# Down-projection's weights scaled and combined ahead, during the FFN, and read back from memory as seven finished quarters

## The chip, the cores and the metric

One core of a Trainium2 chip runs the kernel. The time is the device time of one execution in microseconds. Three runs of the kernel before gave 1437.60, 1434.86 and 1437.55 us, a median of 1437.55 us. One more execution was profiled; its own numbers stand further down.

## What is computed

One decoder layer on x of 1024 tokens by 1024 features: attention of two head groups, an output projection with a residual, then the FFN and a last norm. Only the end of it is touched:

```
h2 = rmsnorm(x, g_ffn) * (1 + sc2) + sh2
gate, up = split(h2 @ w_gu, 2)                    # w_gu: 1024 x 5632
x = x + ga2 * ((silu(gate) * up) @ w_down)        # w_down: 2816 x 1024, ga2: one factor per output column
return rmsnorm(x, g_final)
```

The factor ga2 scales output columns, so it can be multiplied into w_down's columns ahead of the product. All is in float32; every matrix product is made of three matmuls on a high and a low part of each operand.

## The kernel before

**The FFN.** Row blocks f = 0 to 21 (22 blocks of 128 of the 2816 hidden features). Each f makes seven products of quarter size instead of eight (a Strassen-Winograd form): 7 products of 4 x 3 matmuls of 128x512, so 84 per f. `ff_prep(f)` loads the two weight tiles of f (SP queue, L1247, four raw buffers in turn in f16), makes the combinations t1 to t4 on POOL (L1278, L1279, L1282, L1286, into f8) and splits seven operands into high (ACT, L1240) and low (DVE, L1241) parts, in twenty pages used in turn. The products are taken out of PSUM by DVE (L1298 to L1312, one input in PSUM) and ACT (L1297); PSUM has four banks "mm", two "tp" and two "o", and four of the seven products use "mm", two "tp", one "o". POOL makes the two gated results (L1310, L1313) and sends them to memory (L1311, L1314, `spill_g`).

**The down-projection.** First `plain()`, the row blocks 0 and 1 (96 matmuls). Then three chunks `CH` of 3, 3 and 4 pairs of row blocks, each again as seven products (numbered 1, 2, 7, 5, 6, 4, 3 in order of time) of 4 tiles x 3 matmuls x 3 or 4 pairs. `g_quarter` loads quarters of the gated result, `w_quarter` loads quarters b11, b21, b12, b22 of w_down (SP queue, L1353) and multiplies them by ga2 (`scaled`, L1398, on POOL or DVE as the letters of `EN` say). `sub` (L1451, POOL or DVE by `EN`) makes the combinations of both sides: per chunk four of the gated result and four of the weights. `operands` splits the two operands of a product into a high part (ACT, L1365) and a low part (DVE, L1366) in a ring of two places, so the operands of one product are split while PE works on the product before. DVE takes the products out of PSUM and adds them up (L1376).

**What sets the order.** The statements are written in one order; a scheduler that replays the program against its own idea of how long things take decides in which order each engine gets its instructions. On the chip each engine and each DMA queue then runs its list strictly in that order.

In the diff, G is POOL, V is DVE, A is ACT and nc.sync is SP's DMA queue. `mrs` are two buffers of the output projection, f2 one more; all three are unused in the FFN before.

## Time and profile before

| | |
|---|---|
| median of three runs | 1437.55 us |
| the profiled execution, its own time | 1437.92 us |
| its span, first to last instruction | 1436.1 us |
| norms end, FFN begins | about 705 to 755 us |
| FFN at an even pace | about 760 to 1146 us |
| first matmul of the down-projection | 1165.36 us |
| its last matmul | about 1418 us |
| last norm's outputs written | to 1436 us |

PE is the engine that multiplies, with its weight loads (PEld) beside it; busy times overlap between engines, so the busy share of one engine says little without what it waits for. A row of the timeline has a start, a duration that includes any blocking inside the instruction, and in brackets the idle time before it with what ended it. "Granted clock" is 1.00 at 2.4 GHz and 0.50 at 1.2 GHz.

### The profile page before, as it was taken

Reading aid. Unit: us, or ns where it says so; the run is one execution under the profiler, and the core shown is the slowest. Engines: PE = TensorE matmul, PEld = TensorE weight load, DVE = VectorE, ACT = ScalarE, POOL = GpSimd, SP = SyncE. Lnnn points to the kernel's source line nnn. Section 1 sums busy time; section 2 is a strip of 40 time slices with the busy share of each in tenths; the row PEclk is TensorE's granted clock in tenths of the full one; section 3 lists DMA queues with packets and bytes.
Section 4 is the critical chain, followed back from the end, with each engine's and each line's share of the span. In section 5 each row is a group of like instructions: output and inputs, shape, how many; then the busy total and the mean of one; then the engine's idle time right before and its main releaser. Section 6 shows DMA issues by size and latency. Waiting matters only on the chain.

```text
span 1436.1 us, 20358 instructions
## 1 busy us (share of the span) xinstructions
PE 1297.0 (90%) x7477; PEld 1033.9 (72%) x7477; DVE 1016.3 (71%) x1754; ACT 598.8 (42%) x1217; POOL 674.9 (47%) x454
## 2 busy tenths in 40 slices
PE   2999898999878899999869999999999998888894
PEld 0566776798666677787748888888888886766773
DVE  4136899999887477644987545554545569999997
ACT  3435546461456565613763333333333223223334
POOL 1650311324330598122676444445544436487865
PEclk9999898999989999999979999999999999999997
DMA  9723124233311444273423222222223281404004
GB/s 240 238 75 117 30 67 125 91 101 95 126 52 54 147 142 119 76 227 114 161 79 98 89 88 81 66 88 81 81 88 96 87 322 46 154 23 154 0 1 118
DMA packets 133018, 152.11 MB, mean 106 GB/s; under 512 B 9715, under 2 KB 95540, under 8 KB 132918
## 3 DMA queue, kind: packets, MB, share of 16 engines
q1 hardware_dynamic: 122160, 129.56, 29.8%
q0 software_dynamic: 4672, 15.73, 2.9%
q10 hardware_dynamic: 6086, 5.52, 1.5%
q8 instruction: 59, 0.97, 0.3%
q14 instruction: 41, 0.34, 0.1%
HBM read 115.65 MB, written 34.60 MB: 105 GB/s over the span
## 4 chain that ended last, share of the span: by engine, by line
PE 49%; DVE 29%; POOL 8%; DMA 6%; issue 5%; ACT 3%; SPq 1%; DVEq 0%; ACTq 0%; POOLq 0%
DVE score L620 7%; PE mm L1258 6%; PE mm L1256 6%; PE mm L1257 6%; PE tp L1256 3%; PE tp L1258 3%; PE tp L1257 3%; PE mm L366 3%; PE mm L368 3%; PE mm L367 2%; PE o L762 2%; DVE yacc L1376 2%; PE mm L762 2%; PE tp L762 2%; DVE score L424 2%
## 5 line engine op out<-in xcount | busy, mean ns | idle before, releaser
L1240 ACT ACTIVATE wo<-f 128x512 fp32r<-128x512 f32 x124 | 78.0, 631 | 178.0 <-PE mm L1258 78.8
L1241 DVE TENSOR_TENSOR wo<-f,wo 128x512 fp32r<-128x512 f32 x124 | 102.7, 831 | 43.8 <-ACT wo L1240 41.9
L366 PE MATMUL mm<-hh,wl 128*128 128x512 f32 (+2 forms) x288 | 111.7, 389 | 0.0
L367 PE MATMUL mm<-hh,wh 128*128 128x512 f32 (+2 forms) x288 | 111.2, 387 | 0.0
L368 PE MATMUL mm<-hl,wh 128*128 128x512 f32 (+2 forms) x288 | 108.1, 385 | 0.0
L214 POOL TENSOR_SCALAR wh<-wraw 128x1024 fp32r<-128x1024 f32 (+1 forms) x20 | 20.3, 1032 | 132.6 <-PE mm L368 82.3
L366 PE MATMUL mm<-wo,wo 128*128 128x512 f32 x148 | 59.0, 398 | 10.1 <-DVE wo L1366 10.1
L215 POOL TENSOR_TENSOR wl<-wraw,wh 128x1024 fp32r<-128x1024 f32 (+1 forms) x22 | 52.6, 2410 | 29.8 <-ACT ry L144 29.7
L366 PEld LDWEIGHTS mm<-hh,wl 128*128 128x128 f32 (+1 forms) x288 | 54.4, 189 | 15.2 <-issue 2.8
L368 PEld LDWEIGHTS mm<-hl,wh 128*128 128x128 f32 (+1 forms) x288 | 53.7, 188 | 14.0 <-issue 2.2
L367 PEld LDWEIGHTS mm<-hh,wh 128*128 128x128 f32 (+1 forms) x288 | 54.6, 190 | 11.5 <-issue 1.1
L368 PE MATMUL mm<-wo,wo 128*128 128x512 f32 x148 | 56.9, 393 | 1.7 <-DVE wo L1366 1.7
L367 PE MATMUL mm<-wo,wo 128*128 128x512 f32 x148 | 58.2, 393 | 0.0
L793 ACT ACTIVATE ttB<-ttB,mn 128x128 f32<-128x128 f32 (+7 forms) x64 | 49.1, 768 | 15.5 <-DVE mn L789 14.9
L1366 DVE TENSOR_TENSOR wo<-f,wo 128x1536 fp32r<-128x1536 f32 (+1 forms) x17 | 55.1, 3246 | 0.0
L1310 POOL TENSOR_TENSOR f<-f 128x512 f32<-128x512 f32 x15 | 19.8, 1322 | 74.2 <-ACT f L1309 74.2
L366 PE MATMUL mm<-wo,ml 128*128 128x512 f32 x128 | 51.6, 403 | 1.8 <-DVE ml L1109 1.8
L762 PE MATMUL tp<-ident,ttB 128*128 128x128 f32 x288 | 43.6, 294 | 10.2 <-ACT ptB L808 9.7
L620 DVE TENSOR_SCALAR_CACHE_REDUCE score<-kl,sc 128x1024 bf16<-128x1024 uint16 (+2 forms) x48 | 52.3, 1140 | 0.0
L620 DVE TENSOR_SCALAR_CACHE_REDUCE score<-ka,sc 128x768 bf16<-128x768 int16 (+2 forms) x48 | 52.3, 1139 | 0.0
L367 PE MATMUL mm<-wo,mh 128*128 128x512 f32 x128 | 51.0, 398 | 0.0
L368 PE MATMUL mm<-wo,mh 128*128 128x512 f32 x128 | 50.9, 398 | 0.0
(469 smaller groups left out, 4238.7 us busy)
## 6 DMA issues: line engine op xcount, KB each, us to landing
f<-in_w_gu_dram SPq DMA_DIRECT2D x44, 512.0 KB, 3.8
spg<-f POOLq DMA_DIRECT2D x44, 256.0 KB, 2.8
wraw<-in_w_in_dram SPq DMA_DIRECT2D x21, 512.0 KB, 4.0
f<-spg SPq DMA_DIRECT2D x33, 256.0 KB, 3.0
va<-in_w_ada_dram SPq DMA_DIRECT2D x16, 512.0 KB, 4.2
wlm<-in_w_ada_dram SPq DMA_DIRECT2D x32, 256.0 KB, 2.7
f<-in_w_down_dram SPq DMA_DIRECT2D x23, 256.0 KB, 3.1
more<-in_w_down_dram SPq DMA_DIRECT2D x21, 256.0 KB, 5.4
```

The source lines that it names most:

```text
L215: G.tensor_tensor(lo, raw, hi.bitcast(F32), op=OP.subtract)
L366: PE.matmul(p, al, bh, start=(j == 0), stop=False)
L367: PE.matmul(p, ah, bh, start=False, stop=False)
L368: PE.matmul(p, ah, bl, start=False, stop=(j == n - 1))
L620: V.tensor_scalar(mask(t, u), keys[:, seg[t]], z[:, i:i + 1], 0.0, op0=OP.is_lt, op1=OP.add, accum_out=cnt[:, i:i + 1])
L762: pe_last[0] = op(*args, **kw)
L1240: A.activation(h_, src, AF.Copy)
L1241: V.tensor_tensor(l_, src, h_.bitcast(F32), op=OP.subtract)
L1256: PE.matmul(p, w[1][:, k], a[0][:, k], start=(k == 0), stop=False)
L1257: PE.matmul(p, w[0][:, k], a[0][:, k], start=False, stop=False)
L1258: PE.matmul(p, w[0][:, k], a[1][:, k], start=False, stop=(k == 3))
L1366: V.tensor_tensor(l_, x, h_.bitcast(F32), op=OP.subtract)
```

## The change

During the FFN, from f = 1 on, row pairs 1 to 10 of w_down are treated in 40 units (`units`: pair j, and one of four strips h of 128 columns of each half). A unit is loaded by two DMAs of 128 KB on SP's queue into one of three buffers (`wslot`: two of `mrs`, and f2) with four blocks b12, b22, b11, b21 of 128x128; DVE multiplies it by ga2 in two instructions of 128x256; three of the blocks go to `spill_w` (192 KB); POOL makes T3, T2, T1, T4 in place with four subtractions of 128x128, of which the first overwrites b11; the four go to `spill_w` (256 KB). Then the buffer may be loaded again. The down-projection reads b11, b21, T3, T1, T2, T4 and b22 of each chunk, as seven finished quarters, through four buffers in turn (`wq`). `scaled` is gone; of `sub` the four on the gated result remain.

```diff
+    spill_w = {j: dram.tile([P, 7, 512], F32, name=f"spw{j}") for j in range(1, NF // 2)}
...
+    wbuf = [y.rearrange("p a b -> p (a b)") for y in mrs] + [f2]
+    units = [(j, h) for j in range(1, NF // 2) for h in range(4)]
...
+    def w_load(s):
+        if s < len(units):
+            j, h = units[s]
+            for i, u in enumerate((1, 0)):
+                nc.sync.dma_start(wslot(s)[0][:, i], wdn[2 * j:2 * j + 2, :, u * 512 + h * P:u * 512 + h * P + P]
+                                  .rearrange("r p c -> p r c"))
+    def w_step(s):
+        w_load(s + 1)
+        if 1 <= s <= len(units):
...
+            G.tensor_tensor(b11, b12, b11, op=OP.subtract)
+            G.tensor_tensor(b12, b22, b12, op=OP.subtract)
+            G.tensor_tensor(b22, b22, b11, op=OP.subtract)
+            G.tensor_tensor(b21, b21, b22, op=OP.subtract)
+            nc.sync.dma_start(spill_w[j][:, 3:7, h * P:h * P + P], b)
+        if s < len(units):
+            j, h = units[s]
+            for i, u in enumerate((1, 0)):
+                v = wslot(s)[0][:, i]
+                V.tensor_tensor(v, v, gate2[:, u:u + 1, h * P:h * P + P].to_broadcast([P, 2, P]), op=OP.mult)
+            nc.sync.dma_start(spill_w[j][:, 0:3, h * P:h * P + P], wslot(s)[1][:, 1:4])
...
     for f in range(NF):
+        if f:
+            w_step(2 * f - 2)
...
+        if f:
+            w_step(2 * f - 1)
+        else:
+            w_load(0)
...
-    EN = ("GVVVVGGGGGGG", "GGVGGGGGGGGG", "GGGGGGGGGGGG")
+    EN = ("VGGG", "GGGG", "GGGG")
+    wq = [[f6[1], more[:, 13:14]], [more[:, 0:4]], [more[:, 4:8]], [f16[:, 4:8]]]
+    w_todo = [(n, c) for c in CH for n in ("b11", "b21", "T3", "T1", "T2", "T4", "b22")]
+    def w_quarter():
+        name, (j0, j1) = w_todo[nw[0]]
+        nw[0] += 1
+        return quarter(wq[(nw[0] - 1) % 4], lambda j: spill_w[j0 + j][:, w_at[name]], j1 - j0)
...
-    def scaled(q, cs, eng, n):
-        for (v,) in parts(n, q):
-            eng.tensor_tensor(v, v, ga[:, 1:2, cs].to_broadcast([P, v.shape[1], 512]), op=OP.mult)
...
-        sub(b11, b12, b11)
-        sub(b12, b22, b12)
-        sub(b11, b22, b11)
-        sub(b21, b21, b11)
-        o4 = operands(g22, b21)
+        o4 = operands(g22, t4)
```

**SP's queue in the FFN.** In the kernel before, it holds the weight loads (f_6484 is f16, the raw buffers) and nothing else up to the 43rd of the 44 loads; the row ahead of them is the last load of the norms:

```order
L1169 DMA f_6484<-spy_112 128x1024
L1247 DMA f_6484<-in_w_gu_dram 128x8x128 x43
L1353 DMA f_6484<-spg_114 128x512
L1247 DMA f_6484<-in_w_gu_dram 128x8x128
```

In the changed kernel (f16 is f_6494) the same queue carries the units, whose buffers are mr_4722, mr_4723 and f_6500 (f2), and spw is `spill_w`. Twelve rows of the middle of the FFN:

```order
L1248 DMA f_6494<-in_w_gu_dram 128x8x128 x2
L1318 DMA spw_136<-mr_4723 128x4x128
L1305 DMA mr_4723<-in_w_down_dram 128x2x128 x2
L1318 DMA spw_137<-mr_4722 128x4x128
L1318 DMA spw_137<-f_6500 128x4x128
L1248 DMA f_6494<-in_w_gu_dram 128x8x128
L1324 DMA spw_137<-mr_4723 128x3x128
L1305 DMA mr_4722<-in_w_down_dram 128x2x128 x2
L1305 DMA f_6500<-in_w_down_dram 128x2x128 x2
L1324 DMA spw_138<-mr_4722 128x3x128
L1324 DMA spw_137<-f_6500 128x3x128
L1248 DMA f_6494<-in_w_gu_dram 128x8x128
```

What moved: each weight load of the FFN now stands behind loads and stores of units, and all 40 units stand ahead of the last 18 of the 44 weight loads.

**POOL and DVE in the FFN.** POOL's list for one f in the kernel before (f_6485 is f8, f_6486 and f_6487 are f6):

```order
L1282 TENSOR_TENSOR f_6485<-f_6484 128x512
L1278 TENSOR_TENSOR f_6485<-f_6484 128x512
L1279 TENSOR_TENSOR f_6485<-f_6484,f_6485 128x512
L1286 TENSOR_TENSOR f_6485<-f_6484,f_6485 128x512
L1310 TENSOR_TENSOR f_6487<-f_6487 128x512
L1311 DMA spg_116<-f_6487 128x512
L1313 TENSOR_TENSOR f_6486<-f_6486 128x512
L1314 DMA spg_116<-f_6486 128x512
```

POOL in the changed kernel, where f_6495 is f8:

```order
L1314 TENSOR_TENSOR mr_4722<-mr_4722 128x128
L1314 TENSOR_TENSOR f_6500<-f_6500 128x128
L1279 TENSOR_TENSOR f_6495<-f_6494 128x512
L1315 TENSOR_TENSOR mr_4722<-mr_4722 128x128
L1315 TENSOR_TENSOR f_6500<-f_6500 128x128
L1280 TENSOR_TENSOR f_6495<-f_6494,f_6495 128x512
L1316 TENSOR_TENSOR mr_4722<-mr_4722 128x128
L1316 TENSOR_TENSOR f_6500<-f_6500 128x128
L1287 TENSOR_TENSOR f_6495<-f_6494,f_6495 128x512
L1317 TENSOR_TENSOR mr_4722<-mr_4722 128x128
L1317 TENSOR_TENSOR f_6500<-f_6500 128x128
```

DVE in the changed kernel (f_6496 and f_6497 are f6; wo and ml are pages), from behind the multiplications of one pair of units to the first of the next:

```order
L1338 TENSOR_TENSOR f_6497<-mm,f_6497 128x512
L1242 TENSOR_TENSOR wo_6499<-f_6495,wo_6499 128x512
L1340 TENSOR_TENSOR f_6497<-mm,f_6497 128x512
L1242 TENSOR_TENSOR wo_6499<-f_6494,wo_6499 128x512
L1343 TENSOR_TENSOR f_6496<-tp,f_6497 128x512
L1344 TENSOR_TENSOR f_6497<-tp,f_6497 128x512
L1242 TENSOR_TENSOR ml_4725<-f_6494,mh_4724 128x512
L1347 TENSOR_TENSOR f_6497<-o,f_6497 128x512
L1242 TENSOR_TENSOR ml_4727<-f_6495,mh_4726 128x512
L1323 TENSOR_TENSOR mr_4723<-mr_4723,ga 128x256 x2
L1351 TENSOR_TENSOR f_6497<-mm,f_6497 128x512
L1323 TENSOR_TENSOR mr_4722<-mr_4722,ga 128x256
```

What moved: the subtractions of two units stand between POOL's t1 to t4 of an f, and DVE's multiplications of units between the products that it takes out of PSUM. From the first multiplication of the tenth unit to the last of the fortieth, DVE's list holds eight f.

**POOL at the first chunk of the down-projection.** Before (f_6487 and more hold weight quarters, f_6484 is f16):

```order
L1398 TENSOR_TENSOR f_6487<-f_6487,ga 128x1536
L1451 TENSOR_TENSOR more<-f_6487,more 128x1536
L1398 TENSOR_TENSOR more<-more,ga 128x512
L1451 TENSOR_TENSOR f_6486<-f_6486,more 128x1536
L1451 TENSOR_TENSOR f_6484<-more,f_6484 128x1536
L1451 TENSOR_TENSOR f_6485<-f_6485,f_6484 128x1536
L1451 TENSOR_TENSOR f_6484<-f_6487,f_6484 128x1536
L1451 TENSOR_TENSOR more<-more,f_6484 128x1536
L1398 TENSOR_TENSOR f_6484<-f_6484,ga 128x1536
```

After (the last of the FFN, then the subtractions on the gated result alone):

```order
L1350 DMA spg_134<-f_6497 128x512
L1352 TENSOR_TENSOR f_6496<-f_6496 128x512
L1353 DMA spg_134<-f_6496 128x512
L1493 TENSOR_TENSOR f_6496<-f_6496,more 128x1536
L1493 TENSOR_TENSOR f_6494<-more,f_6494 128x1536
L1493 TENSOR_TENSOR f_6495<-f_6495,f_6494 128x1536
L1493 TENSOR_TENSOR f_6494<-f_6494,f_6496 128x1536
L1493 TENSOR_TENSOR f_6496<-f_6496,more 128x1536
```

What moved: the multiplications by ga2 (L1398) and the subtractions of weight quarters are gone from POOL's list, which has 13 subtractions left for the three chunks.

## Rows read from the trace of the kernel before

**Rows 1.** stages: span (us), busy PE, PEld, DVE, ACT, POOL; clock, DMA share, GB/s

```profile
705.00:755.00 50.00, 33.52 (x140) 25.65 (x139) 45.49 (x62) 33.63 (x71) 36.38 (x26) 0.80 0.35 105
760.00:1146.00 386.00, 386.00 (x1669) 313.76 (x1668) 201.83 (x278) 121.97 (x198) 189.40 (x162) 1.00 0.27 84
...
1165.00:1187.00 22.00, 22.00 (x99) 18.20 (x98) 17.37 (x16) 1.16 (x1) 7.79 (x5) 1.00 1.01 374
1187.00:1245.00 58.00, 47.50 (x187) 37.96 (x186) 57.95 (x46) 18.10 (x16) 33.71 (x9) 0.88 0.21 70
```

**Rows 2.** PE's waits, 1150 us to the end: us in total, times, longest

```profile
PE tp L366 <- DVE A11l L1366: 14.8, 4, 6.1
PE mm L366 <- DVE wo L1366: 10.1, 4, 3.9
PE tp L368 <- DVE AS2l L1366: 3.8, 2, 3.1
PE mm L368 <- DVE wo L1366: 1.7, 1, 1.7
```

**Rows 3.** the same columns as the first group, 5 us around long waits

```profile
1200.00:1205.00 5.00, 5.00 (x12) 3.95 (x13) 5.00 (x6) 1.63 (x2) 2.60 (x2) 0.50 0.01 3
...
1225.00:1230.00 5.00, 4.77 (x12) 3.80 (x13) 5.00 (x8) 0.08 (x1) 3.51 (x1) 0.56 0.47 157
```

**Rows 4.** PE in time: first and thirteenth matmul of the down-projection; start, us

```profile
1165.36 0.39 PE L366 MATMUL mm<-AS2h,A11l 128*128 128x512 f32 x1
...
1168.08 0.39 PE L366 MATMUL tp<-AS2h,A11l 128*128 128x512 f32 x1
```

**Rows 5.** DVE in time, down-projection: start, us, engine, line, what

```profile
1193.11 1.74 DVE L1366 TENSOR_TENSOR AS2l<-more,AS2h 128x1536 fp32r<-128x1536 f32 x1
1194.78 4.99 DVE L1366 TENSOR_TENSOR A11l<-f,A11h 128x1536 fp32r<-128x1536 f32 x1
...
1225.10 3.67 DVE L1376 TENSOR_TENSOR yacc<-mm,yacc 128x512 f32<-128x512 f32 x6
```

**Rows 6.** POOL in time, the same stretch

```profile
1182.35 3.49 POOL L1398 TENSOR_TENSOR f<-f,ga 128x1536 f32<-128x1536 f32 x1 [12.43 <-DMA f<-in_w_down_dram]
1193.40 4.74 POOL L1451 TENSOR_TENSOR more<-f,more 128x1536 f32<-128x1536 f32 x1 [7.57 <-DVE f L1451]
...
1223.64 4.87 POOL L1451 TENSOR_TENSOR more<-more,f 128x1536 f32<-128x1536 f32 x1
```

**Rows 7.** DVE's instructions of L1366 alone, in one stretch

```profile
1187.00:1418.00 231.00, 133.94 (x42) 0.96 0.17 57
```

**Rows 8.** instructions of L1451 alone, DVE's and then POOL's

```profile
1187.00:1418.00 231.00, 3.48 (x2) 109.14 (x26) 0.96 0.17 57
```

**Rows 9.** instructions of L1398 alone, DVE's and then POOL's

```profile
1187.00:1418.00 231.00, 6.29 (x3) 35.57 (x8) 0.96 0.17 57
```

**Rows 10.** PE in time, FFN: first matmuls of two neighbouring products

```profile
1045.82 0.39 PE L1256 MATMUL mm<-AS4h,wo 128*128 128x512 f32 x1
...
1048.61 0.39 PE L1256 MATMUL mm<-A11h,wo 128*128 128x512 f32 x1
```

**Rows 11.** POOL's groups in the FFN: busy us, mean ns, idle before

```profile
L1279 POOL TENSOR_TENSOR f<-f,f 128x512 f32<-128x512 f32 x19 | 25.0, 1315 | 1.5
...
L1313 POOL TENSOR_TENSOR f<-f 128x512 f32<-128x512 f32 x13 | 22.5, 1729 | 0.3
```

**Rows 12.** DMA issues: count, KB each, median us to landing

```profile
f<-in_w_gu_dram SPq DMA_DIRECT2D x44, 512.0 KB, 3.8
...
spg<-f POOLq DMA_DIRECT2D x44, 256.0 KB, 2.8
...
more<-in_w_down_dram SPq DMA_DIRECT2D x21, 256.0 KB, 5.4
...
out_dram<-more SPq DMA_DIRECT2D x16, 128.0 KB, 2.1
```

**Rows 13.** SP's issues of L1247: ns each (least, median, most), first and last start

```profile
L1247 SPq DMA_DIRECT2D f<-in_w_gu_dram x44: 367/368/373, 705.9 to 1100.2; - x44
```

More of the change, by code (lines that the diff above doesn't have):

```diff
@@ L1289, in ff_prep, with wslot @@
         return w11, w21, w1, w2, w3, w4, w22
+    wbuf = [y.rearrange("p a b -> p (a b)") for y in mrs] + [f2]
+    units = [(j, h) for j in range(1, NF // 2) for h in range(4)]
+    gate2 = ga[:, 1].rearrange("p (u c) -> p u c", u=2)
+    def wslot(s):
+        return wbuf[s % 3].rearrange("p (u r c) -> p u r c", u=2, r=2), wbuf[s % 3].rearrange("p (a c) -> p a c", c=P)
+    def w_load(s):
[7 more added lines that the diff above has]
+        if 1 <= s <= len(units):
+            j, h = units[s - 1]
+            b = wslot(s - 1)[1]
+            b12, b22, b11, b21 = [b[:, i] for i in range(4)]
+            G.tensor_tensor(b11, b12, b11, op=OP.subtract)
[9 more added lines that the diff above has]
+            nc.sync.dma_start(spill_w[j][:, 0:3, h * P:h * P + P], wslot(s)[1][:, 1:4])
+    w_at = {"b22": 0, "b11": 1, "b21": 2, "T3": 3, "T2": 4, "T1": 5, "T4": 6}
     for f in range(NF):
@@ L1322, in hybrid_block @@
     CH = [(1, 4), (4, 7), (7, 11)]
-    EN = ("GVVVVGGGGGGG", "GGVGGGGGGGGG", "GGGGGGGGGGGG")
+    EN = ("VGGG", "GGGG", "GGGG")
     more = rw.tile([P, 14, 512], F32, name="more")
-    dq = {"g11": [f16[:, 0:4]], "b11": [f16[:, 4:8]], "g12": [f8], "b21": [more[:, 0:4]], "b12": [more[:, 4:8]],
-          "g22": [more[:, 8:12]], "g21": [f6[0], more[:, 12:13]], "b22": [f6[1], more[:, 13:14]]}
+    dq = {"g11": [f16[:, 0:4]], "g12": [f8], "g22": [more[:, 8:12]], "g21": [f6[0], more[:, 12:13]]}
+    wq = [[f6[1], more[:, 13:14]], [more[:, 0:4]], [more[:, 4:8]], [f16[:, 4:8]]]
+    w_todo = [(n, c) for c in CH for n in ("b11", "b21", "T3", "T1", "T2", "T4", "b22")]
+    nw = [0]
     u2s = [dn.tile([P, 512], F32, name=f"u2{i}") for i in range(4)]
@@ L1441, in g_quarter @@
             return quarter(dq[f"g{u + 1}{r + 1}"], lambda j: spill_g[2 * (j0 + j) + r][:, (lo, hi)[u]], j1 - j0)
-        def w_quarter(r, u):
-            q = quarter(dq[f"b{r + 1}{u + 1}"], lambda j: wdn[2 * (j0 + j) + r][:, (lo, hi)[u]], j1 - j0)
-            scaled(q, (lo, hi)[u], next(e), j1 - j0)
-            return q
         def sub(dst, x, y, op=OP.subtract):
@@ L1457, in sum_up @@
             half_final(i)
[L1459 to L1460 removed]
+        g11, b11 = g_quarter(0, 0), w_quarter()
+        g12, b21 = g_quarter(1, 0), w_quarter()
+        g21, t3 = g_quarter(0, 1), w_quarter()
+        g22, t1 = g_quarter(1, 1), w_quarter()
         o1 = operands(g11, b11)
         o2 = operands(g12, b21)
+        t2, t4 = w_quarter(), w_quarter()
         product(1, o1, first)
[L1464 removed]
         sub(g11, g11, g21)
[L1466 to L1468 removed]
         sub(g21, g21, g22, OP.add)
[L1470 removed]
+        o7 = operands(g11, t3)
+        b22 = w_quarter()
         product(2, o2, first)
[L1472 removed]
+        o5 = operands(g21, t1)
         sub(g11, g22, g11)
[L1474 removed]
         product(7, o7, first)
[L1476 removed]
+        o6 = operands(g11, t2)
         product(5, o5, first)
[L1478 removed]
         sub(g12, g12, g11)
[L1480 removed]
+        o4 = operands(g22, t4)
         product(6, o6, first, sum_up if last else None)
```

7 lines of the change are left out of this document (removed).

## Prediction

> **What bounds the kernel now.** I read the busy times by stage first. In the FFN PE is busy for all of 386.0 us at clock 1.00, with DVE at 201.8 and POOL at 189.4 us beside it [rows 1]: work put there on DVE and POOL is free as long as PE never waits. In the down-projection it is the other way round: from 1187 to 1245 us DVE is busy for 57.95 of 58 us, PE for 47.5 [rows 1]. Then PE's waits: 14.8 + 10.1 + 3.8 + 1.7 = 30.4 us in 11 waits, every one ended by DVE's low part of an operand (L1366) [rows 2]. Some of them also halve the granted clock for the next five microseconds (0.50 and 0.56, 12 matmuls in each [rows 3], where five microseconds at a full pace hold 22). A check by counting: from 1187 us to the last matmul at 1418 us are 231 us; the three chunks are 7 x 4 x 3 x (3 + 3 + 4) = 840 matmuls, and at 2.72 / 12 = 0.227 us each [rows 4] they need 190.5 us. So 40.5 us of this stage are lost.
>
> Why DVE is late is seen by laying its rows on POOL's. A low part of 128x1536 takes 1.74 us; the next one, started at 1194.78 us while POOL was in its instruction of 1193.40 us, takes 4.99 us and ends 1.63 us after POOL's [rows 5, 6]. POOL's own instruction of that size takes 3.49 us alone, and 4.74 us when DVE's low part is ahead of it [rows 5, 6]. So an instruction with two SBUF inputs on one of the two engines keeps the other's out for its whole length. DVE's additions from PSUM are not touched: six take 3.67 us, 0.61 us each, beside a POOL instruction [rows 5, 6]. In the whole stretch 42 low parts take 133.9 us [rows 7]; alone, 28 of three blocks at 1.74, 12 of four blocks at 2.3 (by size) and two small ones would take 77.5 us. 56 us of DVE's time are blocking.
>
> **The change part by part.**
>
> *The down-projection.* POOL now does 26 instructions of L1451 for 109.1 us and 8 of L1398 for 35.6 us there, 145 us [rows 8, 9]. After, 13 subtractions remain: 9 of three blocks at 3.49, two of four at 4.65 (by size), two of one block at 1.3 [rows 6, 11], 43 us. DVE also loses three multiplications (6.3 us [rows 9]). What is then late next: a product of three pairs takes PE 36 x 0.227 = 8.2 us; DVE needs two low parts and 40 / 7 additions in that time, 2 x 1.74 + 5.7 x 0.61 = 7.0 us, so it keeps up with 1.2 us to spare; with four pairs it is 10.9 against 8.1 us. A subtraction of 3.5 us that meets a low part makes it late by up to 2.3 us. If all 13 do, 27 us of waits stay (7 x 2.3 + 6 x 1.8); the low parts fill 3.5 / 8.2 = 43% of the time, so I keep 10 us. Gain: 40.5 - 10 = **30 us**, with bounds of 13 and 40 us. The loads go up from 8 to 11 quarters per chunk, but the DMA share of 0.21 there [rows 1] leaves room, and with four buffers each quarter is asked for three products ahead, some 25 us against the longest landing row of 5.4 us [rows 12]. Ahead of product 1 the DMA engines are full (share 1.01, 374 GB/s [rows 1]), and b11's last two blocks now stand behind 4.2 MB of x on SP's queue: 11 us later they land, some 10 us before product 1 begins, so I count no wait.
>
> *The start of the FFN.* The order puts the multiplications of seven units, 14 instructions, ahead of DVE's first FFN result. A 128x256 one is not in the trace; a sixth of 1.74 us and a start-up make 0.33 us (an estimate). DVE is busy for 45.5 of 50 us there [rows 1], so I take all of 14 x 0.33 as **+5 us**; bounds 0 (its idle 4.5 us) and +10 (if the 28 subtractions on POOL, busy for 36.4 of 50 us [rows 1], block as much again).
>
> *The FFN at its even pace.* By amount it fits: 40 x 2 x 0.33 = 26 us on DVE and 160 subtractions on POOL, 0.5 us each (1.315 us for 512 columns [rows 11], 3.49 for 1536 [rows 6], so 0.27 per 128 and 0.5 for the first), 80 us, over some 250 us. What may not fit is the **chain of one unit**, because the queues are in order and the scheduler packed three units into less than one f. Before a buffer can be loaded again there come, one after another: two loads (0.37 us for the first issue [rows 13] and 2.1 us for 128 KB [rows 12]), two multiplications (0.7), the store of three blocks (2.5, between 2.1 for 128 KB and 2.8 for 256 KB [rows 12]), for the first subtraction overwrites b11, then eight subtractions of two units with three of the FFN's own among them (8 x 0.5 + 3 x 1.3 = 7.9), the store of four blocks (2.8), and three issues of others on SP (1.1): 17.5 us. With 0.1 us of blocking for each of the 11 POOL instructions, 18.6 us for every three units (three buffers). The order gives them less: 31 units, the tenth to the fortieth, stand in eight f of DVE's list, and an f is 7 products of 2.79 us [rows 10], 19.5 us; 156 us for ten turns of three, 15.6 us each. So every turn falls 3.0 us behind, and 10.3 turns 31 us. Who waits: a multiplication whose load has not landed holds up DVE's list, in which the next PSUM results stand; PE feels it when a PSUM bank comes round, one f later: 19.5 - 2.8 for filling it - 0.7 for emptying it = 16 us of slack. **+15 us**. Bounds: nothing if a turn takes 17.1 us or less, +39 us at 21 us. SP's weight loads, queued behind the units' stores, have more slack: pages are split about nine products ahead, 25 us.
>
> *Small transfers.* The FFN's weight loads, in 512 B packets too, move 512 KB in 3.8 us [rows 12], and a DMA share of 0.27 moved 84 GB/s [rows 1], so 311 GB/s at a full share; the units add 31 x 0.72 MB in 156 us, 143 GB/s, a share of 0.46: no limit. The Trainium skill's page "DMA: Bandwidth & Descriptors" ("Rules for kernel authors") says to gather small transfers into large ones, and its table of measured bandwidths gives 32% of peak at 64 KB against 78% at 1 MB. By that ratio the units would take a share of up to 1.1, beyond what is left. The rows speak for the first; the other is the last rival below.
>
> *Sum against the profiled 1437.9 us*: -30 + 5 + 15 = -10 us, 1427.9 us; the median of the runs lies 0.4 us lower, so **1427.5 us**.
>
> **The rivals.**
> 1. *The units stay hidden.* If a turn takes at most 17.1 us, the 16 us of slack cover all of it: -30 + 5 = -25, 1412.5 us. For it: the unblocked sum is 17.5 us, and turns with one unit alone have no neighbour among its four subtractions. Against: blocking at the port is in every row of DVE and POOL that overlap.
> 2. *The units set the FFN's pace (slower).* The place is DVE's list between the PSUM results, the price 10.3 us for each microsecond that a turn takes above 17.1 us. It decides from 19.9 us on, where the loss of 28 + 5 us outweighs the gain. At 21 us: +39 + 5 - 30 = +14, 1451.5 us. For it: POOL waits for a store inside its list, with t1 to t4 behind it; L1313 already takes 1.73 us for 1.3 us of work [rows 11]. Against: my sum lies 1.3 us below the point.
> 3. *The down-projection keeps its waits.* The three or four subtractions per chunk hit the low parts each time, or the list places a low part late: gain 13 instead of 30, +7, 1444.5 us. Against: DVE has 22% of the stage to spare.
> 4. *The transfers crowd each other.* Landing takes the 5.4 us seen where the DMA engines were full [rows 12] instead of 2.1 to 2.8, three times per turn, +9 us: 10.3 x 12 - 16 = +108 us, some 1520 us. Against: the share of 0.27 + 0.46. (The skill's rule on small transfers would bring this about.)
>
> **How the numbers follow.** Chances: forecast 0.44 (its own range 1420 to 1436 us), rival 1 0.25, rival 2 0.21, rival 3 0.07, rival 4 0.03. Of 0.2% (about what a measurement can tell, 2.9 us) the bounds are 1434.7 and 1440.4 us. Faster: 0.37 of the forecast and all of rival 1, 0.62. Same: 0.06 of the forecast and 0.02 of rival 3, 0.08. Slower: the rest, 0.30. The range from 1411 us (most of rival 1) to 1453 us (two thirds of rival 2) leaves out about 0.2.
>
> **What would show each step.** Right: from the first chunk to the last matmul about 200 us, low parts of 128x1536 near 2 us on the mean, no clock of 0.50 there; in the FFN gaps of PE ended by DVE's PSUM results, from the third or fourth f on, ending when the fortieth unit is done, some 15 us in all, with DVE waiting for DMA landings of units. Rival 1: no PE gap in the FFN. Rival 2: gaps of 4 us and more per f, and a clock below 1.00. Rival 3: PE waits on L1366's successor above 20 us. Rival 4: unit loads landing later than 4 us. Wrong altogether would be a down-projection in which PE waits for quarters from memory.

## The result and the profile after

The changed kernel takes 1454.5 us (median of 4 runs, 1453.4 to 1457.1) where the kernel before took 1437.6 on the same chip: a ratio of 1.0113, 95% interval 1.0076 to 1.0151. It is slower, and the forecast was 1427.5 us, faster. Ten more runs of it (e11) gave 1448.8 us, a ratio of 1.004, so the loss is some 0.4% to 1.1%.

Three points in the traces cut both kernels into the pieces that the prediction had terms for: VectorE's first addition of the last norms, its first result from the FFN's PSUM, and its result of the last FFN product (line `ff_mm(w22, ...)` of the last f). Here is that last line's group in the kernel before, then in the changed one (duration in ns least/median/most, first and last start in us):

```profile
L1312 DVE TENSOR_TENSOR f<-mm,f x22: 678/691/693, 759.2 to 1165.6; 128x512 f32<-128x512 f32 x22
```

```profile
L1351 DVE TENSOR_TENSOR f<-mm,f x22: 677/688/693, 779.9 to 1217.9; 128x512 f32<-128x512 f32 x22
```

| piece, us of the profiled run | before | after | difference | forecast (bounds) |
|---|---|---|---|---|
| start to the norms' first addition | 666.7 | 673.0 | +6.3 | 0 |
| norms to the FFN's first result | 83.5 | 94.2 | +10.7 | +5 (0, +10) |
| first to last FFN result | 415.4 | 450.7 | +35.3 | +15 (0, +39) |
| last FFN result to the end | 270.5 | 233.9 | -36.6 | -30 (-40, -13) |
| span | 1436.1 | 1451.8 | +15.7 | -10 |

So the down-projection gave what was hoped and a little more, and the units cost 46 us in place of 20. The first 6.3 us lie ahead of any unit; run e11 takes them up.

Stages of the changed kernel (columns as in [rows 1]); the fourth is followed by the same stretch of the kernel before. The last two rows are of the down-projection and of its low parts; they answer to the down-projection's row in [rows 1], 52 us later since the FFN ends later, and to [rows 7]:

```profile
705.00:755.00 50.00, 26.02 (x106) 19.83 (x106) 48.73 (x68) 30.13 (x69) 37.26 (x38) 0.71 0.51 156
730.00:760.00 30.00, 14.13 (x44) 10.49 (x44) 30.00 (x41) 15.84 (x35) 24.59 (x23) 0.55 0.42 122
760.00:1146.00 386.00, 360.71 (x1512) 287.63 (x1512) 234.79 (x326) 108.84 (x188) 258.70 (x295) 0.98 0.49 144
840.00:1000.00 160.00, 136.47 (x546) 105.64 (x545) 96.61 (x144) 36.72 (x67) 114.58 (x154) 0.96 0.59 174
```

```profile
840.00:1000.00 160.00, 160.00 (x693) 130.06 (x692) 81.56 (x116) 51.18 (x83) 77.91 (x67) 1.00 0.25 80
```

```profile
1239.00:1297.00 58.00, 56.27 (x247) 46.02 (x246) 53.32 (x52) 22.14 (x18) 12.59 (x4) 1.00 0.50 164
```

```profile
1220.00:1437.00 217.00, 97.45 (x45) 1.00 0.40 135
```

From 730 to 760 us VectorE is busy all the time and TensorE for less than half of it, at a granted clock of 0.55, mostly the lower level of 1.2 GHz. In the FFN, where TensorE had been busy for 386.0 of 386 us [rows 1], 25 us are missing, nearly all between 840 and 1000 us. Idle time is not all of it: TensorE did 546 matmuls in those 160 us, 693 in the kernel before, which is about 34 us of work, and it was idle for 23.5 us; the other 10 us or so are matmuls that took longer, 0.250 us on the mean against 0.231, at a granted clock of 0.96. Whether a full clock would have won them back, no run shows. In the down-projection TensorE is busy for 56.3 of 58 us (47.5 before), the clock is 1.00, and the low parts of operands take 97 us in place of 134 [rows 7].

TensorE's waits from 660 to 1250 us (in all, times, longest):

```profile
PE mm L1257 <- DVE f L1351: 9.5, 5, 3.1
PE tp L1187 <- DVE rm L157: 9.4, 1, 9.4
PE tp L1187 <- DVE f L1180: 8.8, 2, 6.1
PE tp L1257 <- DVE f L1344: 8.4, 4, 4.0
PE tp L1257 <- DVE f L1337: 3.3, 2, 2.1
```

The lines that end on L1351, L1344 and L1337 are PSUM results of the FFN: a bank comes free late. The two of L1187 are the last norms' transposes. VectorE's own waits, from 680 to 1250 us, and TensorE's from 1218 us to the end:

```profile
DVE mr L1323 <- DMA mr<-in_w_down_dram: 46.0, 20, 4.9
...
DVE f L1323 <- DMA f<-in_w_down_dram: 17.9, 8, 7.8
```

```profile
PE mm L367 <- DVE wo L1417: 1.9, 2, 1.1
PE tp L367 <- DVE A11l L1417: 1.7, 1, 1.7
```

VectorE stands for 63.9 us in 28 waits in front of L1323, the units' multiplication, because a unit's load has not landed. In the down-projection TensorE waits for 3.6 us, against 30.4 in [rows 2].

**One stall followed.** The changed kernel from 927 to 949 us; first SyncE's issues and GpSimd, then VectorE, then TensorE (start, us, engine, line, what, and what ended the idle time before it):

```profile
927.36 0.89 SPq L1305 DMA_DIRECT2D f<-in_w_down_dram  x2
...
931.99 0.37 SPq L1324 DMA_DIRECT2D spw<-f  x1
...
939.67 0.36 SPq L1318 DMA_DIRECT2D spw<-f  x1
942.77 0.89 SPq L1305 DMA_DIRECT2D f<-in_w_down_dram  x2
```

```profile
935.17 0.53 POOL L1314 TENSOR_TENSOR f<-f 128x128 f32<-128x128 f32 x1 [2.95 <-DMA spw<-f]
...
939.16 0.48 POOL L1317 TENSOR_TENSOR f<-f 128x128 f32<-128x128 f32 x1
```

```profile
930.56 1.40 DVE L1323 TENSOR_TENSOR f<-f,ga 128x256 f32<-128x256 f32 x2 [0.59 <-DMA f<-in_w_down_dram]
...
936.71 0.68 DVE L1340 TENSOR_TENSOR f<-mm,f 128x512 f32<-128x512 f32 x1
945.19 0.54 DVE L1323 TENSOR_TENSOR f<-f,ga 128x256 f32<-128x256 f32 x1 [7.80 <-DMA f<-in_w_down_dram]
...
947.45 0.68 DVE L1344 TENSOR_TENSOR f<-tp,f 128x512 f32<-128x512 f32 x1
```

```profile
948.18 0.80 PE L1257 MATMUL tp<-AS1h,wo 128*128 128x512 f32 x1 [4.03 <-DVE f L1344]
```

A buffer's turn, from one load to the next, can be read off: loaded at 927.4, multiplied at 930.6, first store issued at 932.0 and landed when GpSimd goes on at 935.2, four subtractions (with others among them) up to 939.6, second store at 939.7, next load at 942.8, multiplied at 945.2. VectorE had nothing to do but wait from 937.4 to 945.2, with the PSUM result of L1344 three places behind in its list; TensorE stood until that was read, and its first matmul behind the pause took 0.80 us where [rows 10] have 0.39 (granted clock 0.82 from 945 to 950 us). The turn shown took 15.4 us and is one of the shorter ones: ten turns of this buffer from 781 to 979 us took 13.0 to 28.0 us, 19.7 on the mean. The Trainium skill's page "PSUM — Partial Sum Buffer" ("Engine vs sequencer instructions") says that VectorE's queue is strictly first in, first out; these rows show what that means here.

The spacing of the 22 results of L1351 gives the pace: 19.4 us, then seven f of 29.0, 26.5, 25.4, 26.1, 23.0, 26.1 and 23.7, then 16.9, 13.5 and 13.9, and from there 19.4 to 19.5. VectorE's list holds 28 units in those seven f, four in each. Against the 19.45 us of an f in the kernel before they run 43.6 us late, and the three behind them catch up 14.0.

### The profile page after: what moved, and what is told of

Read it like the earlier page. It is cut to its first block, busy times and chain, and to the rows that moved or that the text cites. A ratio compares the mean times of both kernels' runs of the same rounds, so it can differ in the third digit from the quotient of the medians.

```text
span 1451.8 us, 20937 instructions
## 1 busy us (share of the span) xinstructions
PE 1305.5 (90%) x7477; PEld 1038.0 (71%) x7477; DVE 1027.8 (71%) x1831; ACT 591.6 (41%) x1218; POOL 667.1 (46%) x591
## 5 line engine op out<-in xcount | busy, mean ns | idle before, releaser
L1242 DVE TENSOR_TENSOR wo<-f,wo 128x512 fp32r<-128x512 f32 x124 | 116.8, 945 | 20.8 <-ACT wo L1241 19.8
L1323 DVE TENSOR_TENSOR mr<-mr,ga 128x256 f32<-128x256 f32 x54 | 32.6, 621 | 62.1 <-DMA mr<-in_w_down_dram 46.0
L369 PEld LDWEIGHTS mm<-hl,wh 128*128 128x128 f32 (+1 forms) x288 | 53.7, 188 | 13.9 <-issue 2.2
L1339 ACT ACTIVATE f<-f 128x512 f32<-128x512 f32 x22 | 13.9, 633 | 106.9 <-DVE f L1338 106.6
L1493 POOL TENSOR_TENSOR f<-f,f 128x1536 f32<-128x1536 f32 (+1 forms) x5 | 21.5, 4295 | 65.7 <-DVE wo L1417 33.5
L425 DVE SCALAR_TENSOR_TENSOR score<-rl,wi,score 128x512 f32<-128x512 f32 (+2 forms) x70 | 48.1, 742 | 4.2 <-ACT rl L419 3.3
```

The costliest lines, as they stand in the source:

```text
L369: PE.matmul(p, ah, bl, start=False, stop=(j == n - 1))
L425: V.scalar_tensor_tensor(sc, rl, w, sc, op0=OP.mult, op1=OP.add)
L1242: V.tensor_tensor(l_, src, h_.bitcast(F32), op=OP.subtract)
```

## The experiments

Ratios are to the kernel before on the same chip, with 95% intervals. The table has the three pieces from above, in us of each profiled run; "norms" is from the norms' first addition to the first FFN result. One edit carries most of the runs. Without it, the scheduler packs the units as early as their buffers allow. The **pacing edit** ties a unit's loads to SyncE's queue behind the weight loads of the f in whose text they stand, so that the loop's text sets the number of units per f:

```diff
-        nc.sync.dma_start(raw, wgu[:, :, col:col + P])
+        gu_last[0] = nc.sync.dma_start(raw, wgu[:, :, col:col + P])
...
-                nc.sync.dma_start(wslot(s)[0][:, i], ...)
+                with tc.issue_after(gu_last[0].ins):
+                    nc.sync.dma_start(wslot(s)[0][:, i], ...)
```

| run | what | us | ratio | norms | FFN | rest |
|---|---|---|---|---|---|---|
| before | | 1437.6 to 1442.4 | 1 | 83.5 | 415.4 | 270.5 |
| after | | 1454.5 | 1.0113 (1.0076 to 1.0151) | 94.2 | 450.7 | 233.9 |
| e1 | no multiplications | 1422.9 | 0.986 (0.9818 to 0.9902) | 85.8 | 428.9 | 234.1 |
| e2 | no subtractions in the units | 1422.3 | 0.9858 (0.9827 to 0.9888) | 92.6 | 424.9 | 233.9 |
| e3 | 2 units per f | 1411.8 | 0.9793 (0.975 to 0.9836) | 90.8 | 416.0 | 234.4 |
| e4 | no units | 1405.9 | 0.9745 (0.9716 to 0.9775) | 83.5 | 415.4 | 234.6 |
| e5 | 2 per f, later | 1406.7 | 0.976 (0.9735 to 0.9786) | 85.3 | 414.7 | 234.0 |
| e6 | 3 per f | 1450.6 | 1.006 (1.004 to 1.0079) | 87.6 | 456.1 | 234.4 |
| e7 | 4 per f | 1448.5 | 1.0051 (1.0034 to 1.0069) | 87.6 | 454.2 | 234.3 |
| e8 | multiplications on GpSimd | 1420.0 | 0.985 (0.9826 to 0.9874) | 86.5 | 428.0 | 234.0 |
| e9 | GpSimd work put back, short | 1437.4 | 0.995 (0.9929 to 0.9972) | 85.3 | 414.8 | 265.7 |
| e10 | e5 with two buffers | 1407.0 | 0.9743 (0.9709 to 0.9778) | 85.3 | 414.8 | 234.1 |
| e11 | the changed kernel again | 1448.8 | 1.004 (1.0017 to 1.0063) | 94.2 | 451.3 | 234.2 |
| e12 | GpSimd work put back, long | 1428.8 | 0.9917 (0.9887 to 0.9948) | 85.4 | 414.8 | 257.0 |
| e13 | no sums in the down-projection | 1401.6 | 0.9731 (0.9693 to 0.977) | 85.4 | 414.7 | 229.2 |

**e1_no_scale.**

```diff
-                V.tensor_tensor(v, v, gate2[:, u:u + 1, h * P:h * P + P].to_broadcast([P, 2, P]), op=OP.mult)
```

> Leaves out the 80 multiplications with the gate that VectorE does in the units; the units still load, subtract, store, and the down-projection reads them (so its weights are unscaled). In the changed kernel the FFN lasts 438.0 us from its first to its last VectorE result on the last product's line, against 406.4 before, and VectorE waits 63.9 us in 28 waits for the units' loads ahead of these multiplications. Theory A (VectorE stands in its list in front of a multiplication whose load has not landed, and the PSUM results behind it hold TensorE up): the FFN falls to 406 to 412 us and the time to about 1454.5 - 29 = 1425 us, or to 1418 if the multiplications also hold up the norms ahead of the FFN. Rival B (GpSimd's 160 subtractions, their waits for the first store and the shared port hold the FFN up): the FFN stays at 430 to 438 us, the time at 1447 to 1454 us.

The FFN from its first to its last result on the last product's line took 413.3 us, 1.3 us above theory A's range, and the time is 1422.9: theory A's case, but not the whole of the loss. Seven f still take 21.2 to 25.3 us each. And the norms' piece falls from 94.2 to 85.8 us, but the first f then takes 15.6 us to its last result in place of 12.7: from the norms' first addition to there it is 101.4 us, against 106.9 in the changed kernel and 92.5 before, so the multiplications account for 5.5 of the 14.4 us that are lost at the start.

**e2_no_subs.**

```diff
-            G.tensor_tensor(b11, b12, b11, op=OP.subtract)
-            G.tensor_tensor(b12, b22, b12, op=OP.subtract)
-            G.tensor_tensor(b22, b22, b11, op=OP.subtract)
-            G.tensor_tensor(b21, b21, b22, op=OP.subtract)
```

> Leaves out the 160 subtractions of the units on GpSimd; loads, multiplications and both stores stay (so the combined weights are not combined). Theory A (VectorE's waits for the units' loads): VectorE's waits in front of the multiplications stay, over fewer products since a unit's turn is shorter; the FFN takes 420 to 438 us and the time is 1437 to 1454 us. Rival B (GpSimd's subtractions and the port): the FFN falls to 406 to 412 us and the time to 1420 to 1428 us.

412.8 us and 1422.3 us: here it is B's number, though e1 had refuted B. Without subtractions a buffer's turn is shorter, the units are through in the fifth f (80 multiplications, 30 of them ahead of the first f's last result), and the lateness of four f (23.2 to 26.6 us each) is caught up as in the changed kernel. Taking out either step shortens the turn and most of the loss goes; neither theory, as a matter of one engine's work, was right. What is left is the length of the turn against the time that an f gives it, and the next runs go by that.

**e3_paced.** The pacing edit alone.

> Changes only the order: each unit's two loads are put on SyncE's queue behind the FFN weight loads of the f in whose text it stands, so that two units run per f in place of up to four; the same work is done. Theory A: with about 29 us for a turn of 18.6 to 19.1 us VectorE's waits for loads shrink from 63.9 us to under 15 us, the FFN takes 406 to 414 us and the time is 1420 to 1428 us (the start of the FFN, with 5 units still ahead of it, keeps 5 to 14 us of its loss). Rival B (the work itself, by port and GpSimd, costs, wherever it stands): the FFN keeps 430 us or more, the time 1446 to 1455 us.

The same work, and 404.0 us on the last product's line, 1411.8 us in all, better than theory A's 1420 to 1428. But its reason fails: VectorE's waits for loads did not shrink, they are 88 us in 25 waits. So it is not the waiting of VectorE as such that costs. Two units per f need less than an f, and 19 of the 25 waits, 72.1 us, stand at one place, behind the fifth PSUM result of an f, where TensorE does not yet need the next one read: it is busy for 385.0 of the 386 us from 760 us. In the changed kernel VectorE's 28 waits stand at six places of an f.

**e4_no_units.**

```diff
-    return quarter(wq[(nw[0] - 1) % 4], lambda j: spill_w[j0 + j][:, w_at[name]], j1 - j0)
+    return quarter(wq[(nw[0] - 1) % 4], lambda j: wdn[2 * (j0 + j) + w_at[name] % 2][:, (lo, hi)[w_at[name] // 2 % 2]], j1 - j0)
...
-            w_step(2 * f - 2)
...
-            w_step(2 * f - 1)
```

> Leaves the 40 units out; the down-projection's quarters are read straight from the weights, unscaled and uncombined, with the same sizes and buffers. It prices the down-projection's half of the change alone. From the profiles of before and after: the stretch from the FFN's last result to the end falls by 36.6 us (270.5 to 233.9), the start and the FFN go back to before's, so 1437.6 - 36.6 = 1401 us; if the 6.3 us by which the changed kernel is late already ahead of the first unit belong to the change, 1407 us. Rival (part of the 36.6 us is not the down-projection's own gain but FFN work that was pushed over the boundary): 1408 to 1415 us.

The first two pieces are before's to a tenth of a microsecond, the last falls by 35.9 us, and the time by 35.7 against before's 1441.6 there. The gain belongs to the down-projection itself, and about 1406 us is what the kernel would take if the units cost nothing.

**e5_late.** The pacing edit, and the units two f later:

```diff
-        if f:
-            w_step(2 * f - 2)
+        if f >= 3:
+            w_step(2 * f - 6)
...
-        if f:
-            w_step(2 * f - 1)
-        else:
+        if f >= 3:
+            w_step(2 * f - 5)
+        elif f == 2:
             w_load(0)
+        if f == NF - 1:
+            for s in range(2 * f - 4, len(units) + 1):
+                w_step(s)
```

> As e3_paced (two units per f, by the place of their loads on SyncE's queue), but the units stand from the fourth f of the text on in place of the second, with three at the end, so that one or two units in place of five lie ahead of the FFN's first result. Theory A (units ahead of the FFN's first results delay the norms on VectorE and GpSimd): from the norms' first addition to the last result of f 0 take 92.5 us in the kernel before and 102.8 us in e3_paced; here 93 to 96 us, so 1411.8 - 8 = 1404 us (1402 to 1407), within 3 us of e4_no_units, which has no unit at all. Rival B (that loss comes from something else in the changed order): still 102 us, 1410 to 1413 us.

1406.7 us, within a microsecond of the kernel without units. From the norms to the first f's last result it is 96.8 us (92.5 before), a little above the 93 to 96 that were expected, and the FFN gives most of that back. TensorE in the FFN, and VectorE's waits from 700 to 1250 us:

```profile
760.00:1146.00 386.00, 386.00 (x1669) 313.81 (x1668) 296.53 (x359) 110.53 (x199) 289.69 (x318) 1.00 0.54 157
```

```profile
DVE mr L1325 <- DMA mr<-in_w_down_dram: 60.0, 14, 6.5
DVE f L1325 <- DMA f<-in_w_down_dram: 24.9, 6, 4.6
```

Nearly all of the units' work lies in a window in which TensorE does not pause, with a DMA share of 0.54 and 84.9 us of waits of VectorE, 18 of the 20 behind the fifth result. This version beats both kernels by 2.4% and more.

**e6_three.** The pacing edit with three steps per f from f = 2 on.

> As e3_paced with three units per f, from the third f of the text on. In the changed kernel 28 units stood in seven f that took 25.67 us each, 6.42 us per unit. Theory A (the ring of three buffers gives a unit every 6.42 us at best, and VectorE's list is slowed to that): three per f ask for 19.3 us, an f has 19.45 us: FFN 406 to 416 us, time 1404 to 1416 us. Rival B (every unit beyond two per f costs TensorE a wait, about 3 us each): ten f with one such unit each, FFN 430 us or more, 1430 us or more.

Theory A's number falls and the result is in rival B's range: 442.3 us, 1450.6 us; eleven f take 22.0 to 27.0 us, 23.8 on the mean. One f of it, from VectorE and GpSimd:

```profile
906.80 0.76 DVE L1325 TENSOR_TENSOR mr<-mr,ga 128x256 f32<-128x256 f32 x2 [6.20 <-DMA mr<-in_w_down_dram]
```

```profile
909.36 1.35 POOL L1352 TENSOR_TENSOR f<-f 128x512 f32<-128x512 f32 x1 [5.10 <-ACT f L1351]
```

VectorE waits for the loads; the PSUM result behind them comes late, so ScalarE's silu and GpSimd's gate product of it (L1352) do; the twelve subtractions stand behind that product in GpSimd's list, the stores behind the subtractions, and the loads of the next f behind the stores. With each of the three buffers used once per f, an f is as long as that loop. The 6.42 us per unit were not a constant of the ring: the length of a turn depends on what stands around it in the lists.

**e7_four.** The same with four steps per f.

> As e6_three with four units per f, from the third f of the text on, so the packing of the changed kernel without most of its units ahead of the FFN. Theory A: 4 x 6.42 = 25.7 us per f against 19.45, for nine f in a row: 9 x 6.2 = 56 us, less the 14 us that the changed kernel caught up again: FFN 435 to 455 us, time 1404 + 42 = 1446 us (1435 to 1458). Rival B (the changed kernel's loss came from the units ahead of the FFN and the low clock there, and not from the pace): FFN at most 418 us, time at most 1422 us.

440.4 us and 1448.5 us, within A's range. With most units out of the norms the FFN's loss is there in full. Nine f take 222.0 us, 24.7 each and 6.2 per unit.

**e8_pool_mult.**

```diff
-                V.tensor_tensor(v, v, gate2[:, u:u + 1, h * P:h * P + P].to_broadcast([P, 2, P]), op=OP.mult)
+                G.tensor_tensor(v, v, gate2[:, u:u + 1, h * P:h * P + P].to_broadcast([P, 2, P]), op=OP.mult)
```

> The changed kernel with the units' 80 multiplications on GpSimd in place of VectorE, as tightly packed as before; the same result. Theory A (the pace hurts because the wait for a unit's load stands in VectorE's list between PSUM results): the waits move into GpSimd's list, whose sums for the weight pages are made about an f ahead of need, and TensorE's gaps shrink: FFN 406 to 420 us, time 1415 to 1430 us. Rival B (whichever list the ring's pace stands in holds the FFN up): the ring is longer with slower multiplications, FFN 435 us or more, time 1450 us or more.

410.3 us and 1420.0 us: A. GpSimd, which is busy for 328.8 us of the window of 386 (258.7 in the changed kernel), carries more work than in any other run here, and TensorE loses less. What matters is in whose list the wait stands, though not that alone: 12.6 us of the FFN's loss stay.

**e9_pool_back.** e5_late, and behind each subtraction of the first two chunks:

```diff
                 eng.tensor_tensor(*v, op=op)
+                for o, a, b in [(wbuf[j % 3], v[1][:, j], v[2][:, j]) for _ in range(0 if last else 2) for j in range(v[1].shape[1])]:
+                    G.tensor_tensor(o, a, b, op=op)
```

> e5_late, and in the down-projection's first two chunks GpSimd does each of the eight subtractions' reads twice more, 512 columns at a time, into buffers that nobody reads: 48 instructions of about 1.31 us, 63 us, which bring GpSimd from 79 us there to about 142 (it did 145 us of subtractions and scalings in the kernel before). No operand waits for them by data. Theory A (an instruction with two SBUF inputs on GpSimd keeps VectorE's low parts out): the low parts, 97.2 us in 44 in e5_late and 133.9 us in 42 before, go to 120 to 135 us, TensorE waits for them again for 10 to 25 us, and the time is 1406.7 + 10 to 25 = 1417 to 1432 us. Rival B (the gain came from the scalings and differences that no longer stand ahead of an operand, and not from the port): low parts below 105 us, time at most 1410 us.

The time goes up by 30.7 us, more than either theory said, but the low parts only to 103.9 us. One row shows where it went:

```profile
1261.21 1.76 DVE L1422 TENSOR_TENSOR A11l<-f,A11h 128x1536 fp32r<-128x1536 f32 x1 [11.85 <-ACT A11h L1421]
```

VectorE idles for 11.9 us before the second chunk's first operand: the added instructions read the quarters' buffers, which come free late (SyncE's loads wait for them 12 times, 46.8 us). The run does not decide; e12 does the same without holding a buffer.

**e10_two_bufs.** e5_late with one buffer fewer, and a unit's load behind the store that frees its buffer:

```diff
-    wbuf = [y.rearrange("p a b -> p (a b)") for y in mrs] + [f2]
+    wbuf = [y.rearrange("p a b -> p (a b)") for y in mrs]
...
     def w_step(s):
-        w_load(s + 1)
...
             nc.sync.dma_start(spill_w[j][:, 3:7, h * P:h * P + P], b)
+        w_load(s + 1)
```

> e5_late (two units per f) with two buffers for the units in place of three, so that every buffer is used once per f, as in e6_three. There one f took 23.4 us and held one turn of all buffers: loads issued at 902.4 us, multiplied from 906.8 us, the last subtraction at 921 us. Theory A (an f is as long as the turn that stands in it, whose parts per unit, four subtractions of 0.65 us and about 1.5 us of loads, multiplications and issues, add up): 23.4 - 4.1 = 19.3 us, within an f's 19.45: FFN 403 to 412 us, time 1406 to 1416 us. Rival B (without a spare buffer f stretches to about 23.4 us whatever its units are): 17 x 3.9 - 14.5 = 52 us, FFN 450 us or more, 1455 us or more.

1407.0 us and an FFN of 400.7 us on the last product's line (a little under A's 403): A. No spare buffer is needed; a turn of two units fits into an f, one of three does not.

**e11_as_changed.** The changed kernel as it is.

> The changed kernel itself once more, beside the others. Its first profile is 6.3 us late already at the norms' first addition (673.0 us against 666.7), where no unit has begun. Theory A (that is a matter of the execution, as the same point lies between 666.2 and 671.5 us in the runs so far, whose code ahead of it is the same): another value from 666 to 673 us here; from there to the last result of the FFN again some 46 us more than before, and 36 less after it. Rival B (the change itself costs 6 us ahead of the units): 672 us or more again.

After the norms' first addition the pieces are those of the first profile to 0.6 us: +10.7, +35.9, -36.3. That first addition comes at 676.5 us, which by the letter is B's number. But ScalarE and GpSimd have the same instructions in the same order up to 640 us as in e5_late, where that addition came at 669.5, and as in the kernel before; ten executions of this kernel lie between 1442.8 and 1458.0 us, and the profiled one is the slowest of them. So the last pieces are firm, and the 6.3 us ahead of them are most likely the execution's own, which no row proves. The two ratios, 1.0113 and 1.004, differ by some 10 us; the pieces alone say +9.4 us, 1.0065, between them.

**e12_pool_long.** e5_late with long instructions that hold no quarter's buffer:

```diff
+    spare = dn.tile([P, 1536], F32, name="spare")
+    gaf = ga.rearrange("p a b -> p (a b)")
...
-                eng.tensor_tensor(*v, op=op)
+                did = eng.tensor_tensor(*v, op=op)
+            with tc.issue_after(did.ins) if eng is G and not last else nullcontext():
+                for _ in range(2 if eng is G and not last else 0):
+                    G.tensor_tensor(spare, gaf[:, 0:1536], gaf[:, 512:2048], op=op)
```

> e5_late, and in the down-projection's first two chunks GpSimd does two more subtractions of 1536 columns behind each of its seven there, on the gate's and the last norm's weights, which nobody writes, into a buffer of their own: 14 instructions of 3.49 us, 49 us. No operand waits for them by data and no quarter's buffer is held by them, which e9_pool_back's held. Theory A (an instruction with two SBUF inputs on GpSimd keeps a low part out for its whole length): by the blocking per GpSimd time seen so far (56 us in 145 before, 20 us in 79 in e5_late) the low parts grow by 12 to 19 us, from 97.2 to 109 to 116 us; in e9_pool_back, whose instructions were a third as long, they grew by 6.7 us; TensorE waits 5 to 20 us more, time 1412 to 1427 us. Rival B (no port; the operands' chain alone made the gain): low parts 95 to 100 us, time 1404 to 1410 us.

**e13_no_sums.** The other way round, `sub` does nothing:

```diff
-                eng.tensor_tensor(*v, op=op)
+            pass
```

> e5_late with the twelve sums and differences of gate quarters in the down-projection left out (GpSimd's eleven and VectorE's one), so the products use wrong operands of the same sizes. Theory A: with no long instruction on GpSimd beside them the low parts fall from 97.2 us to the 77.5 us that the prediction worked out as their time alone; TensorE, which waits only 3.7 us there, gains 0 to 4 us: 1402 to 1407 us. Rival B (low parts are longer for another reason): 90 us or more.

The low parts from 1165 to 1435 us and the largest of their groups (busy us, mean ns), in e5_late, e12_pool_long and e13_no_sums:

```profile
1165.00:1435.00 270.00, 98.92 (x45) 0.97 0.39 129
...
L1422 DVE TENSOR_TENSOR wo<-f,wo 128x1536 fp32r<-128x1536 f32 x12 | 26.3, 2188 | 0.6 <-ACT wo L1421 0.6
```

```profile
1165.00:1435.00 270.00, 123.68 (x45) 0.94 0.39 131
...
L1424 DVE TENSOR_TENSOR wo<-f,wo 128x1536 fp32r<-128x1536 f32 x12 | 38.7, 3228 | 0.6 <-ACT wo L1423 0.6
...
L1503 POOL TENSOR_TENSOR spare<-ga 128x1536 f32<-128x1536 f32 x14 | 60.5, 4321 | 0.5
```

```profile
1165.00:1435.00 270.00, 82.26 (x45) 0.97 0.39 129
...
L1422 DVE TENSOR_TENSOR wo<-f,wo 128x1536 fp32r<-128x1536 f32 x12 | 21.0, 1750 | 0.6 <-ACT wo L1421 0.6
```

Fourteen instructions of GpSimd on data that no operand needs lengthen the low parts by 24.8 us (12 to 19 expected), make TensorE wait for 19.1 us and cost 22.1 us (1428.8 us, a little above theory A's 1427); taking the sums away brings a low part of 1536 columns back to 1.75 us and the time down by 5.0. VectorE's additions out of PSUM, which have one input in SBUF, take 680 ns on the mean in e5_late and in e12. So it is GpSimd's instructions beside them that hold the low parts up, and not the operands' chain alone. The Trainium skill's page "SBUF — State Buffer" ("Who interferes with whom") says that a VectorE instruction with two inputs in SBUF contends with a GpSimd instruction that reads SBUF; these runs agree, with 2.19 us on the mean beside eleven long sums, 3.23 beside 25 long instructions and 1.75 beside none.

## Why the prediction was wrong

**The down-projection: right in mechanism, a little short in size.** Forecast -30, measured -36.6. The residual waits were taken as 10 us and are 3.6, which is nearly the whole difference. The blocking between the two engines, which the step rests on, is shown by e12 and e13, and the 840 matmuls then run nearly without a pause at clock 1.00, in some 195 us where about 200 were forecast. Rival 3 (the waits stay) is out. Blocking alone, put back in e12, costs 23.0 of the 36.6 us with GpSimd busy for 145.8 us from 1165 to 1435 us, against 178.7 in the kernel before; how the rest divides between blocking and the shorter chain of the operands stays open.

**The start of the FFN: under-sized, and outside its bounds.** Forecast +5, at most +10, measured +10.7. To the last result of the first f it is 14.4 us. The count of 14 multiplications was right, their price of 0.33 us was not: they take 10.65 us, 0.76 each. Six of them took 0.40 to 0.43 us; the rest is most likely time in which GpSimd's instructions beside them kept the others out, which the prediction had as its outer bound only. They wait 3.7 us more for their loads, which the step did not count at all (it had named the wait for the even pace only). VectorE's work of the norms is held up as well: a low part beside GpSimd's instructions, three of the units' subtractions and three of the norms' own in turn, took 5.65 us, where [rows 5] have 1.74 for three times the size.

```profile
715.71 5.65 DVE L1161 TENSOR_TENSOR AS3l<-f,AS3h 128x512 fp32r<-128x512 f32 x1
...
765.23 2.02 DVE L1323 TENSOR_TENSOR f<-f,ga 128x256 f32<-128x256 f32 x2 [3.37 <-DMA f<-in_w_down_dram]
767.17 0.68 DVE L1337 TENSOR_TENSOR f<-tp,f 128x512 f32<-128x512 f32 x1
```

VectorE stands for 3.4 us directly ahead of that first result (767.17). From the norms' first addition to the last result of the first f it is 14.4 us more than in the kernel before, 8.9 more without multiplications (e1), 11.7 with them on GpSimd (e8), 12.2 without subtractions (e2), and 4.3 with one or two units ahead of the FFN in place of seven (e5). So it is the units ahead of the FFN as a whole, and no one engine's share, that cost; how it divides between own time, blocking and waits stays open.

**The FFN's even pace: this is the step that turned the sign.** Forecast +15, measured +35.3; of this 29.6 us are the seven f with four units each (43.6 late, 14.0 caught up), and 5.9 the first two. The place and the direction were right: VectorE's list, with waits for the units' loads between the PSUM results. The step that failed is the price, a turn of 18.6 us for three units against 15.6 us that the order gives it. Three of its terms were off. The order gives less: 156 us divided by 31 / 3 turns are 15.1, not 15.6, and the eight f were not evenly filled; where it hurts there are four units in an f, 14.6 us for three. A turn took 19.25 us there, 25.67 x 3 / 4. And the slack was 14.0 us, not 16. In the prediction's own sum the first makes +21 of +15, the second with it +27, the third +29, and the first two f, which it left out, the rest.

But the 19.25 us are the pace itself put in other words, no second measurement, and e6 shows that the sum is not sound as a form either. There the order gives a turn of three units a whole f, 19.45 us, more than the forecast's 18.6; with that turn nothing would be lost, but a turn took 23.8 and the FFN lost 40.7 us. The prediction added up the links of the chain by their own lengths, with three of the FFN's instructions among GpSimd's subtractions at 1.3 us each, and put at nothing what those wait for. In e6 GpSimd stands idle for 5.1 us in front of the gate product, with the subtractions behind it, since the PSUM result that the product needs stands behind VectorE's wait for a unit's load: the chain closes on itself, and an f becomes as long as the loop. Two units per f leave that loop shorter than an f (e5, e10), three or four do not (e6, e7). How much of the changed kernel's 35.3 us comes from the packing and how much from this lengthening stays open.

**Rival 2 is what happened, but its point of decision was wrong.** It was priced at 1451.5 us for a turn of 21 us and said to decide from 19.9. The turn was 19.25 and the kernel was slower all the same, for the point hung on the same 15.6 us and on +5 for the start. With 14.6 us in place of 15.6 and +10.7 in place of +5 the same sum puts the point 1.6 us lower, below the forecast's own 18.6. Of its signs the clock came (0.98 from 760 to 1146 us); the gaps of TensorE were 25 us in seven f, 3.6 each, where it had 4 and more. At 0.21 it had too small a chance: the sum lay 1.3 us from a point that two of its own estimates could move by more.

**What it had not asked.** The rivals held the mechanism, but the prediction took the packing as part of the work. The same 40 units at two per f cost 1.1 us in all (e5: 500.0 us from the norms to the last FFN result, 498.9 before). Rival 1 is out for the order as it was packed, though another order does hide the work. Rival 4 is out: with a DMA share of 0.49 in the FFN the units' loads landed after 2.7 and 2.9 us (median, 760 to 1000 us), not 5.4, and after 4.2 and 4.3 us in e5, where they cost nothing.

```profile
mr<-in_w_down_dram SPq DMA_DIRECT2D x44, 128.0 KB, 2.7
...
f<-in_w_down_dram SPq DMA_DIRECT2D x24, 128.0 KB, 2.9
```

The rule on small transfers that the prediction cites from the Trainium skill's page "DMA: Bandwidth & Descriptors" ("Rules for kernel authors") decided nothing here: at that share and these times the DMA engines were not the limit.

## What to carry to other kernels

Work that is hidden under another engine is free only if its waits stand in a list where nothing urgent is behind them: count the longest chain through its buffers, with the in-order lists that it passes and what the work in them waits for, against the time that the packed order gives it, not its busy time against idle time. A scheduler that places side work as early as its buffers allow will fill a few stages to the brim; a single ordering edge that spreads it evenly was worth about 3% here with the same work (e3), a little more with a later start (e5), and that even with one buffer fewer (e10). When a sum lies near the point at which a rival wins, work the rival out as carefully as the forecast.

## What the runs showed of the hardware

A VectorE instruction with two inputs in SBUF is held up by GpSimd's, and what it costs does not follow from GpSimd's busy time. In e9 GpSimd did 48 added instructions of 512 columns, 94.1 us, and the low parts grew by 6.7 us (98.9 to 105.6 from 1165 to 1435 us); in e12 it did 14 of 1536 columns, 60.5 us, and they grew by 24.8. In e9 GpSimd lost as well: an instruction of 1.3 us took 1.96 on the mean. The length of GpSimd's instructions is a likely reason and not the whole one: the two runs also differ in the buffers that they hold, and the low part of 5.65 us above, in the changed kernel, stood beside six short GpSimd instructions in a row, 0.45 to 1.29 us each, and ended 0.5 us behind the last of them. Which engine gives way, and when, stays open.

```profile
715.78 0.47 POOL L1315 TENSOR_TENSOR mr<-mr 128x128 f32<-128x128 f32 x1
...
719.54 1.28 POOL L1215 TENSOR_TENSOR f<-f,f 128x512 f32<-128x512 f32 x1
```
